# Loads moved and spread at two places of a hybrid mLSTM and attention decode step: gate columns, constants and sinks at the start, the samples' attention in the middle

## The chip, the cores and the metric

The kernel runs on one core of a Trainium2 chip. The metric is device time in microseconds (us), the median over runs. The engines named below are TensorE (PE for its products, PEld for its weight loads), VectorE (DVE), ScalarE (ACT), GpSimd (POOL) and SyncE (SP, which here issues most DMAs). Each engine runs its own instructions in a fixed order.

## The reference

One layer of a decoder works on 512 prompt tokens and on 8 sampled sequences of 4 tokens: 544 columns of x, each of width 2048. It projects x with one large matrix, runs two branches (an mLSTM with 4 heads of 512, and sliding-window attention with 32 query heads and 4 key heads of 64), gates and merges them and ends in a layer norm:

```
u = einsum('btd,dc->btc', x, w_in)         # q_m k_m v_m o_m z_m q_a k_a v_a z_a g_m g_a i_pre f_pre
ig = i_pre + b_igate ; lf = log_sigmoid(f_pre + b_fgate)
h_m, C, n, m = mlstm(q_m, k_m, v_m, ig, lf, C0, n0, m0)
h_a = softmax([q_a k_a - slope*dist, sink]) v_a      # window of 128; samples read the stored K and V too
br_m = norm(h_m) * sigmoid(o_m) * silu(z_m) ; br_a = h_a * silu(z_a)
y = sigmoid(g_m) * (br_m @ w_proj_m) + sigmoid(g_a) * (br_a @ w_proj_a)
out = layernorm(ALPHA * x + y @ w_out)
```

It also returns the mLSTM states and the new K and V rows, for the prompt and for the samples. i_pre and f_pre, the gate columns, are the last 8 columns of w_in.

## The kernel before

All values are float32. Each operand of a product is split into a high part, a cast to the format that TensorE takes, and a low part, the rest (`split` for weights, lines 193 to 203: the cast on ScalarE at line 200, the subtraction on VectorE at line 201; `hilo` for x and other data, lines 243 to 245). Three products (high by high, high by low, low by high) make one.

**The start.** x comes in five column blocks on SP (line 306), with two halves of the first weights between them (`load_half`, line 187); a third half follows. The 16 slices of x are called pieces here, k = 0 to 15. Each piece is turned by four transposes on TensorE (line 324) and split by `hilo`; for k below 8 a copy (line 331) goes with it. The samples' x lies in the tile `xs`, of which half is used. Then SP issues seven small loads (lines 360 to 366): the rest of the constants `cc`, the two biases, the state m0, the norm's weights, and the attention sinks in two layouts. ScalarE casts parts of the constants into `sel` and `m8r` (lines 369 and 376). Two plain products follow (`gemm`, the attention's values, columns VA_ and VA_ + 128); between the halves of the second, `gates_half` loads 8 gate columns into a tile of the three-buffer weight pool (line 381), casts them twice on ScalarE (lines 386, 387), subtracts on VectorE (line 388) and multiplies (line 393).

**The pairs.** Most of the time goes to `paired`. A pair is two column blocks of weights, worked out together by a scheme with seven half products instead of eight (lines 668 and 670, `half_product`: 16 and 8 products of 272 columns). The seven operands of x are called a11, s1, n2, xk, n3, s4, xk. The weights of a step are prepared three steps ahead.

**Ticks.** Everything beside the pairs is written as generators, held in a list. After each half product `tick()` lets every generator run to its next `yield`; a `yield` thus means "go on one step later". Instructions that a tick issues on TensorE are placed behind the half product just issued. `tc.issue_after(ins)` asks for such a place: what is issued in its block on the engine of `ins` stands behind `ins` there. `state["load"]`, `state["cast"]` and `state["split"]` hold the latest weight load (SP), weight cast (ScalarE) and weight subtraction (VectorE). `tc.high_priority` lets a block be placed ahead of what was written before it. For the rest a planner orders each engine's instructions by what is ready in its own estimate of time.

**From the samples' attention to the attention branch.** `attentions` runs the 16 prompt attentions, then `sample_attention`. It issues 13 loads in a row: z (gas), new keys (kas), values (vas), eight pieces of q (qraw, lines 912 to 918), and the stored K and V (kb and vb, 1 MB each, lines 922 and 923). It yields five times, scales q (line 932), transposes the keys (line 939) and goes on. When it is done, `samples` works through four mLSTM heads of the samples, each a fixed number of yields: eight rounds (line 1226 reads the state, line 1231 updates it) and a tail, `sample_finish`: a product (line 1177), a norm, transposes (line 1184) and a store (line 1186). Right behind the last tail `samples` gives its memory free and loads the 16 blocks of the attention branch into the tiles `pf` (line 1261). When the pairs are done, `branch` splits these blocks (bh and bl, by `hilo`), and the products with w_proj_a begin (line 210).

Of the kernel before, what the change touches and what calls it, by code (L numbers as in the profile page):

```python
# [15 lines left out]
F32 = mybir.dt.float32  # L16
# [58 lines left out]
def _build(tc, nc, i, o, es):  # L75
# [25 lines left out]
    def nm(s):  # L101
        count[0] += 1
        return f"{s}_{count[0]}"
# [120 lines left out]
    def gemm(wv, c0, xh, xl, cols=EVEN, raws=(None, None), every=8, prio=0, before=None, parts=(1, 1),  # L224
             ps=None):
        ps = ps or mm()
        for half in range(2):
            if before:
                before(half)
            raw = raws[half] or load_half(wv, c0, half)  # L230
            if prio:
                with tc.high_priority(offset=prio):
                    wh, wl = split(raw, parts=parts[half])
            else:
                wh, wl = split(raw, parts=parts[half])
            products(ps, half, wh, wl, xh, xl, cols, every)
        return ps
# [5 lines left out]
    def hilo(src, hi, lo, eng=None):  # L243
        A.copy(hi, src)
        (eng or V).tensor_tensor(out=lo, in0=src, in1=r32(hi), op=ALU.subtract)
# [66 lines left out]
    state["load"] = xdma  # L312
    with tc.issue_after(xdma.ins):
        raw0.append(load_half(win, VA_ + 128, 0))
# [4 lines left out]
    for g in range(8):  # L319
        for q in range(2):  # L320
            k = g * 2 + q
            pt = sm()
            for t in range(4):
                PE.transpose(pt[:, t * 128:t * 128 + 128], xt[k][:, t], ident)
# [34 lines left out]
    with tc.issue_after(state["load"].ins):  # L359
        nc.sync.dma_start(cc[:, 128:C_DIST], i["consts"][:, 128:C_DIST])  # L360
        nc.sync.dma_start(bi[:, 0:1], i["b_igate"].unsqueeze(1))
        nc.sync.dma_start(bi[:, 1:2], i["b_fgate"].unsqueeze(1))
        nc.sync.dma_start(m0, i["state_mlstm_m"].rearrange("b h -> h b"))
        nc.sync.dma_start(wn[:], i["mlstm_norm_w"].rearrange("(a p) -> p a", p=128))
        nc.sync.dma_start(sinkb[:], i["attn_sinks"].partition_broadcast(128))
# [3 lines left out]
    A.copy(sel[:], cc[:, C_SEL:C_SEL + 32])  # L369
# [5 lines left out]
    for q in (0, 2):  # L375
        A.copy(m8r[q * 32:q * 32 + 32], cc[q * 32:q * 32 + 32, C_M8:C_M8 + 8])


    def gates_half(ps, half):
        raw = wr.tile([128, 8, 128], F32, tag="raw", name=nm("graw"))  # L380
        nc.sync.dma_start(raw[:, :, 0:8], win[:, half * 8:half * 8 + 8, GI:GI + 8])
        wa, wb = gate_w
        for g in range(2):
            src = raw[:, :, g * 4:g * 4 + 4]
            hi = wa[:, :, g * 32:g * 32 + 4]
            A.copy(hi, src)
            A.copy(wb[:, :, g * 32:g * 32 + 4], src)
            V.tensor_tensor(out=wa[:, :, 64 + g * 32:68 + g * 32], in0=src, in1=r32(hi), op=ALU.subtract)
# [516 lines left out]
    def sample_attention():  # L905
# [9 lines left out]
        for kvh in range(KVH):  # L915
            half = slice((kvh % 2) * 64, (kvh % 2) * 64 + 64)
            for a in range(2):
                nc.sync.dma_start(qraw[half, kvh // 2, a::2],
                                  d_qa[kvh * 4:kvh * 4 + 4, a * 64:a * 64 + 64].rearrange("k p t -> p k t"))
        kb = t1.tile([128, NB, 256], F32, name="kb")  # L920
        vb = t1.tile([128, NB, 256], F32, name="vb")
        nc.sync.dma_start(kb[:], i["state_attn_k"].rearrange("b t k d -> t b (k d)"))
        nc.sync.dma_start(vb[:], i["state_attn_v"].rearrange("b t k d -> t b (k d)"))
# [986 lines left out]
```

## Time and profile before

| | |
|---|---|
| Time, median of 3 runs | 2465.89 us (2465.31 to 2469.09) |
| Profiled execution, own time | 2469.53 us |
| Its span | 2467.7 us |
| Granted TensorE clock, mean | 0.997 |
| PE busy | 2436.4 us (99%) |
| PEld busy | 2379.8 us (96%) |
| DVE busy | 1876.5 us (76%) |
| ACT busy | 1216.6 us (49%) |
| POOL busy | 509.8 us (21%) |
| Data moved | 464.72 MB, mean 188 GB/s |

A row of the order of time gives the start in us, the duration, the engine, the line in the kernel, the operation, the tile written and the tiles read, the shape, and the count of merged instructions; in brackets stands how long the engine had been idle and what it waited for. SPq marks DMA issues on SP, whose duration is that of the issue, not of the transfer. A row of waits gives who waited for whom, the total in us, the number of times and the longest. A row of stretches gives start and end, the length, the busy time and number of instructions of each engine, the granted clock (1.00 is full), the DMA engines' busy share and GB/s. Durations of products overlap, since the engine is pipelined: two products of 272 columns start 0.125 us apart though each shows 0.29 us.

### The profile page before, as it was taken

How to read it: one execution, taken by the hardware profiler on the slowest of the kernel's cores; microseconds unless marked ns; L12 is line 12 of the kernel's file. 1: busy time of each engine (PE TensorE's matmuls, PEld its weight loads, DVE VectorE, ACT ScalarE, POOL GpSimd, SP SyncE). 2: the span in 40 equal slices, each digit the busy share in tenths (PEclk: the TensorE clock that was granted, in tenths of full speed). 3: DMA queues.
4: the chain of work that ended last, by engine and by line, in shares of the span. 5: the costliest groups of instructions: out<-in, count | busy, mean ns of one | idle time of the engine just before them, and what ended most of it. 6: DMA issues, size and time to landing. Idle time of an engine off the chain costs nothing.

```text
span 2467.7 us, 48808 instructions
## 1 busy us (share of the span) xinstructions
PE 2436.4 (99%) x19446; PEld 2379.8 (96%) x19446; DVE 1876.5 (76%) x2813; ACT 1216.6 (49%) x1994; POOL 509.8 (21%) x478
## 2 busy tenths in 40 slices
PE   8999999999999999999999999999999999999997
PEld 8999999999999999999999999999999999999996
DVE  7868888888888887787877878877866654777657
ACT  5456676676576664443433544544633333334431
POOL 3114333333333330121012122111000000110111
PEclk9999999999999999999999999999999999999998
DMA  6776666666666645477678577677755546888875
GB/s 170 192 180 158 164 157 152 158 154 162 154 151 169 151 121 144 122 214 237 192 240 243 177 230 227 180 237 229 243 196 171 178 153 204 227 224 253 222 217 179
DMA packets 557435, 464.72 MB, mean 188 GB/s; under 512 B 45592, under 2 KB 454344, under 8 KB 556952
## 3 DMA queue, kind: packets, MB, share of 16 engines
q1 hardware_dynamic: 540312, 402.09, 54.8%
q0 software_dynamic: 15696, 57.15, 12.1%
q8 instruction: 153, 2.51, 0.4%
q10 hardware_dynamic: 1200, 2.36, 0.3%
q14 instruction: 74, 0.61, 0.1%
HBM read 319.06 MB, written 96.31 MB: 168 GB/s over the span
## 4 chain that ended last, share of the span: by engine, by line
PE 92%; DMA 3%; DVE 2%; SPq 1%; issue 1%; ACT 0%; DVEq 0%; POOL 0%; POOLq 0%
PE bank L668 45%; PE bank L670 22%; PE bank L210 10%; PE sm L1414 2%; PE bank L1226 1%; PE sm L1446 1%; PE sm L778 1%; PE sm L1459 1%; PE sm L824 1%; PE sm L210 1%; DMA tx<-d_y 1%; DMA ty<-d_y 1%; PE sm L1776 1%; DMA raw<-in_w_in 1%; PE sm L804 1%
## 5 line engine op out<-in xcount | busy, mean ns | idle before, releaser
L200 ACT CAST wh<-raw 128x1024 fp32r<-128x1024 f32 x632 | 662.5, 1048 | 843.7 <-PE bank L668 690.1
L201 DVE TENSOR_TENSOR wl<-raw,wh 128x1024 fp32r<-128x1024 f32 x632 | 788.6, 1249 | 203.4 <-ACT wh L200 177.4
L668 PE MATMUL bank<-xk,wh 128*128 128x272 f32 x2336 | 322.7, 289 | 0.0
L648 DVE TENSOR_TENSOR raw<-raw,raw 128x1024 f32<-128x1024 f32 x238 | 302.4, 1271 | 8.3 <-DMA raw<-in_w_in 4.3
L668 PEld LDWEIGHTS bank<-xk,wh 128*128 128x128 f32 x2336 | 302.8, 188 | 3.5 <-issue 2.6
L687 POOL TENSOR_TENSOR ev<-p,ev 128x272 f32<-128x272 f32 x82 | 119.2, 1454 | 435.2 <-ACT ev L686 412.5
L668 PE MATMUL bank<-n3h,wh 128*128 128x272 f32 x656 | 169.5, 291 | 1.6 <-DVE ev L689 1.6
L670 PE MATMUL bank<-xk,wl 128*128 128x272 f32 x1168 | 169.6, 287 | 0.0
L668 PE MATMUL bank<-n2h,wh 128*128 128x272 f32 x656 | 169.5, 291 | 0.0
L668 PE MATMUL bank<-s1h,wh 128*128 128x272 f32 x656 | 169.2, 291 | 0.0
L668 PE MATMUL bank<-n2l,wh 128*128 128x272 f32 x656 | 167.8, 287 | 0.0
L668 PE MATMUL bank<-n3l,wh 128*128 128x272 f32 x656 | 167.7, 288 | 0.0
L668 PE MATMUL bank<-s1l,wh 128*128 128x272 f32 x656 | 167.2, 287 | 0.0
L668 PE MATMUL bank<-s4h,wh 128*128 128x272 f32 x656 | 167.1, 288 | 0.0
L668 PE MATMUL bank<-s4l,wh 128*128 128x272 f32 x656 | 166.8, 287 | 0.0
L670 PEld LDWEIGHTS bank<-xk,wl 128*128 128x128 f32 x1168 | 155.5, 188 | 0.0
L668 PE MATMUL bank<-a11h,wh 128*128 128x272 f32 x584 | 150.3, 289 | 0.0
L668 PE MATMUL bank<-a11l,wh 128*128 128x272 f32 x584 | 149.6, 288 | 0.0
L210 PE MATMUL bank<-bh,wl 128*128 128x272 f32 x704 | 148.5, 289 | 0.0
L210 PE MATMUL bank<-bh,wh 128*128 128x272 f32 x704 | 148.0, 289 | 0.0
L210 PE MATMUL bank<-bl,wh 128*128 128x272 f32 x704 | 146.0, 288 | 0.1
L646 POOL DMA_DIRECT2D raw<-raw x90 | 78.5, 873 | 287.0 <-DVE ev L695 209.8
(492 smaller groups left out, 5668.5 us busy)
## 6 DMA issues: line engine op xcount, KB each, us to landing
raw<-in_w_in SPq DMA_DIRECT2D x296, 512.0 KB
raw<-raw POOLq DMA_DIRECT2D x90, 512.0 KB, 5.0
C<-in_state_mlstm_C SPq DMA_DIRECT2D x32, 1024.0 KB
out<-C SPq DMA_DIRECT2D x64, 512.0 KB
raw<-in_w_proj_a SPq DMA_DIRECT2D x32, 512.0 KB
raw<-in_w_proj_m SPq DMA_DIRECT2D x32, 512.0 KB
raw<-in_w_out SPq DMA_DIRECT2D x32, 512.0 KB
d_v<-ev SPq DMA_DIRECT2D x16, 272.0 KB
```

The lines of the kernel that those rows point to most:

```text
L200: state["cast"] = A.copy(wh[:, k:k + n], raw[:, k:k + n])
L201: state["split"] = V.tensor_tensor(out=wl[:, k:k + n], in0=raw[:, k:k + n], in1=r32(wh[:, k:k + n]), op=ALU.subtract)
L210: PE.matmul(ps[f][:, :w], a[:, kk], b(k, c, w), start=(k == 0 and n == 0), stop=(k == 15 and n == 2))
L646: G.dma_start(out=w[out][:], in_=w[b][:], accum_op=ALU.add)
L648: V.tensor_tensor(out=w[out][:], in0=w[a][:], in1=w[b][:], op=ALU.add)
L668: PE.matmul(ps, wh[:, k], x(p, k), start=(first and k == 0 and p == 0), stop=False, skip_group_check=True)
L670: state["end"] = PE.matmul(ps, wl[:, k], x(0, k), start=False, stop=(k == 7), skip_group_check=True)
L687: G.tensor_tensor(out=c22, in0=p1, in1=c11, op=ALU.subtract)
L778: PE.matmul(pp[:, c0 + w0:c0 + 256], qs[a][:, j * 128:j * 128 + 128], kx[:, k0:k0 + 256 - w0], start=(n == 0), stop=(n == 1))
L804: PE.transpose(pt[:, b * 128:b * 128 + 128], s_[:, b, 128:256], ident)
L824: PE.matmul(po[:, b * 128:b * 128 + n], VA[:, b], p_[:, 2 * b:2 * b + n // 128], start=(b == 0 and m == 0), stop=(b == 3 and m == 1), skip ...
L1414: PE.matmul(pp[:, 0:258], a[:, b * 128:b * 128 + 128], b_[:, b, f], start=(b == 0 and n == 0), stop=(b == 3 and n == 2))
```

## The change

1. The gate columns get a place in the unused half of `xs`. Both loads are issued behind the last block of x and ahead of the third weight half. The gate casts on ScalarE are placed behind the last cast of x.
2. The seven small loads and the casts into `sel` and `m8r` move into a generator, `small_loads`, started after the first plain product: biases, m0 and constants in its first tick, the norm's weights and the sinks three ticks later, the casts three ticks after that. Each is placed behind the latest weight load or weight cast.
3. The first weight cast on ScalarE is placed behind the cast of the piece k = 3.
4. The 13 loads of the samples' attention are spread: kas, vas and gas at once; one pair of q loads in each of the next four ticks; kb and vb in later ticks; then q is scaled, and the key transposes follow two ticks after that. Every load is placed behind the latest weight load, the scaling behind the latest weight subtraction. From the first load to the key transposes there are ten yields, where there were five.

```diff
@@ gemm
-                wh, wl = split(raw, parts=parts[half])
+                with tc.issue_after(behind.ins) if behind and half == 0 else ExitStack():
+                    wh, wl = split(raw, parts=parts[half])
@@ hilo
-        A.copy(hi, src)
+        state["x_cast"] = A.copy(hi, src)
@@ loads of x
+    graw = blk(xs[:, 4], 2)
     with tc.issue_after(xdma.ins):
+        for half in range(2):
+            nc.sync.dma_start(graw[:, half].rearrange("p (k c) -> p k c", c=8), win[:, half * 8:half * 8 + 8, GI:GI + 8])
         raw0.append(load_half(win, VA_ + 128, 0))
@@ pieces of x
+                if k == 3:
+                    state["k3"] = state["x_cast"]
...
+                x_cast = state["x_cast"]
@@ small loads
-    with tc.issue_after(state["load"].ins):
-        nc.sync.dma_start(cc[:, 128:C_DIST], i["consts"][:, 128:C_DIST])
...
-        nc.sync.dma_start(sinkc[:], i["attn_sinks"].unsqueeze(1).to_broadcast([AH, NTS]))
-    A.copy(sel[:], cc[:, C_SEL:C_SEL + 32])
+    def small_loads():
+        with tc.issue_after(state["load"].ins):
+            nc.sync.dma_start(bi[:, 0:1], i["b_igate"].unsqueeze(1))
+            nc.sync.dma_start(bi[:, 1:2], i["b_fgate"].unsqueeze(1))
+            nc.sync.dma_start(m0, i["state_mlstm_m"].rearrange("b h -> h b"))
+            nc.sync.dma_start(cc[:, 128:C_DIST], i["consts"][:, 128:C_DIST])
+        for _ in range(3):
+            yield
+        with tc.issue_after(state["load"].ins):
+            nc.sync.dma_start(wn[:], i["mlstm_norm_w"].rearrange("(a p) -> p a", p=128))
+            nc.sync.dma_start(sinkb[:], i["attn_sinks"].partition_broadcast(128))
+            nc.sync.dma_start(sinkc[:], i["attn_sinks"].unsqueeze(1).to_broadcast([AH, NTS]))
+        for _ in range(3):
+            yield
+        with tc.issue_after(state["cast"].ins):
+            A.copy(sel[:], cc[:, C_SEL:C_SEL + 32])
...
@@ gates_half
-        raw = wr.tile([128, 8, 128], F32, tag="raw", name=nm("graw"))
-        nc.sync.dma_start(raw[:, :, 0:8], win[:, half * 8:half * 8 + 8, GI:GI + 8])
+        raw = graw[:, half].rearrange("p (k c) -> p k c", c=8)
...
-            A.copy(hi, src)
-            A.copy(wb[:, :, g * 32:g * 32 + 4], src)
+            with tc.issue_after(x_cast.ins):
+                A.copy(hi, src)
+                A.copy(wb[:, :, g * 32:g * 32 + 4], src)
@@ plain products
-                  before=gates_between if kk else None, ps=[sm(), sm()] if kk else None)
+                  before=gates_between if kk else None, ps=[sm(), sm()] if kk else None, behind=state["k3"])
...
+            spawn(small_loads())
@@ sample_attention
-        nc.sync.dma_start(gas[:], d_bra[:, :, SEQ:T].rearrange("k p t -> p k t"))
-        nc.sync.dma_start(kas[:], d_ka[:, :, SEQ:T].rearrange("k p t -> p k t"))
-        nc.sync.dma_start(vas[:], d_vr[SEQ:T])
...
+        with tc.issue_after(state["load"].ins):
+            nc.sync.dma_start(kas[:], d_ka[:, :, SEQ:T].rearrange("k p t -> p k t"))
+            nc.sync.dma_start(vas[:], d_vr[SEQ:T])
+            nc.sync.dma_start(gas[:], d_bra[:, :, SEQ:T].rearrange("k p t -> p k t"))
...
-        for _ in range(5):
-            yield
-        for j in range(2):
-            V.tensor_scalar(qas[:, j], qraw[:, j].rearrange("p g (b t) -> p b g t", t=NTS), 0.125, None, op0=ALU.mult)
+        for kvh in range(KVH):
+            half = slice((kvh % 2) * 64, (kvh % 2) * 64 + 64)
+            yield
+            with tc.issue_after(state["load"].ins):
+                for a in range(2):
+                    nc.sync.dma_start(qraw[half, kvh // 2, a::2],
+                                      d_qa[kvh * 4:kvh * 4 + 4, a * 64:a * 64 + 64].rearrange("k p t -> p k t"))
+        for t_, src in ((kb, i["state_attn_k"]), (vb, i["state_attn_v"])):
+            yield
+            with tc.issue_after(state["load"].ins):
+                nc.sync.dma_start(t_[:], src.rearrange("b t k d -> t b (k d)"))
+            yield
+        with tc.issue_after(state["split"].ins):
+            for j in range(2):
+                V.tensor_scalar(qas[:, j], qraw[:, j].rearrange("p g (b t) -> p b g t", t=NTS), 0.125, None, op0=ALU.mult)
+        for _ in range(2):
+            yield
```

More of the change, by code (lines that the diff above doesn't have):

```diff
@@ L224, in gemm @@
     def gemm(wv, c0, xh, xl, cols=EVEN, raws=(None, None), every=8, prio=0, before=None, parts=(1, 1),
-             ps=None):
+             ps=None, behind=None):
         ps = ps or mm()
@@ L357, in t5 @@
         return t544.tile([128, n], dt, tag="t544", name=nm("t"))
-    with tc.issue_after(state["load"].ins):
-        nc.sync.dma_start(cc[:, 128:C_DIST], i["consts"][:, 128:C_DIST])
[L361 to L365, printed above, removed]
-        nc.sync.dma_start(sinkc[:], i["attn_sinks"].unsqueeze(1).to_broadcast([AH, NTS]))
     G.memset(mh[:], -0.5)
     V.tensor_scalar(ones_r[:], cc[:, 0:2], 0.0, 0.5, op0=ALU.mult, op1=ALU.add)
-    A.copy(sel[:], cc[:, C_SEL:C_SEL + 32])
     for t_ in (row_h, nM):
@@ L374, in _build @@
     V.memset(r32(m8r[:]), 0.0)
-    for q in (0, 2):
-        A.copy(m8r[q * 32:q * 32 + 32], cc[q * 32:q * 32 + 32, C_M8:C_M8 + 8])
+    def small_loads():
[14 more added lines that the diff above has]
+            A.copy(sel[:], cc[:, C_SEL:C_SEL + 32])
+            for q in (0, 2):
+                A.copy(m8r[q * 32:q * 32 + 32], cc[q * 32:q * 32 + 32, C_M8:C_M8 + 8])
     def gates_half(ps, half):
-        raw = wr.tile([128, 8, 128], F32, tag="raw", name=nm("graw"))
-        nc.sync.dma_start(raw[:, :, 0:8], win[:, half * 8:half * 8 + 8, GI:GI + 8])
+        raw = graw[:, half].rearrange("p (k c) -> p k c", c=8)
         wa, wb = gate_w
@@ L911, in sample_attention @@
         vas = t1.tile([32, 256], F32, name="vas")
-        nc.sync.dma_start(gas[:], d_bra[:, :, SEQ:T].rearrange("k p t -> p k t"))
-        nc.sync.dma_start(kas[:], d_ka[:, :, SEQ:T].rearrange("k p t -> p k t"))
-        nc.sync.dma_start(vas[:], d_vr[SEQ:T])
[L915 to L919, printed above, removed]
+        with tc.issue_after(state["load"].ins):
+            nc.sync.dma_start(kas[:], d_ka[:, :, SEQ:T].rearrange("k p t -> p k t"))
+            nc.sync.dma_start(vas[:], d_vr[SEQ:T])
+            nc.sync.dma_start(gas[:], d_bra[:, :, SEQ:T].rearrange("k p t -> p k t"))
         kb = t1.tile([128, NB, 256], F32, name="kb")
         vb = t1.tile([128, NB, 256], F32, name="vb")
-        nc.sync.dma_start(kb[:], i["state_attn_k"].rearrange("b t k d -> t b (k d)"))
-        nc.sync.dma_start(vb[:], i["state_attn_v"].rearrange("b t k d -> t b (k d)"))
         E = t1.tile([128, NB, 132], F32, name="E")
```

## The prediction

> **What bounds the kernel now.** I read the page's totals first, then a table of stretches, then the waits of TensorE, then the order of time on single engines around each place the diff touches.
>
> ```profile
> span 2467.7 us, 48808 instructions
> PE 2436.4 (99%) x19446; PEld 2379.8 (96%) x19446; DVE 1876.5 (76%) x2813; ACT 1216.6 (49%) x1994; POOL 509.8 (21%) x478
> ```
>
> TensorE is busy in all but 31.3 us of the span, so a change that keeps its products can win only where TensorE stands idle, and loses wherever a new idle stretch opens. The stretches (columns: length, busy time of PE, PEld, DVE, ACT, POOL, granted clock, DMA share, GB/s) say where the idle time lies:
>
> ```profile
> 8.00:12.20 4.20, 2.74 (x21) 2.27 (x19) 0.49 (x2) 1.51 (x3) 0.00 (x0) 1.00 1.08 366
> 12.20:20.00 7.80, 7.02 (x54) 6.62 (x55) 6.47 (x18) 7.05 (x25) 6.19 (x5) 1.00 1.10 350
> 20.00:30.00 10.00, 6.59 (x51) 5.90 (x50) 6.04 (x14) 4.58 (x18) 5.06 (x4) 1.00 0.36 35
> 40.00:50.00 10.00, 10.00 (x82) 10.00 (x82) 10.00 (x18) 4.11 (x8) 0.00 (x0) 1.00 0.54 144
> ...
> 920.00:930.00 10.00, 9.69 (x78) 9.51 (x77) 5.11 (x7) 3.55 (x4) 1.41 (x1) 1.00 0.53 123
> 930.00:940.00 10.00, 9.05 (x99) 8.70 (x98) 5.25 (x7) 2.03 (x4) 0.00 (x0) 1.00 1.11 317
> 940.00:950.00 10.00, 9.15 (x132) 8.39 (x134) 8.87 (x14) 6.56 (x14) 2.97 (x2) 1.00 0.30 90
> ...
> 1760.00:1765.00 5.00, 4.94 (x39) 4.67 (x38) 4.59 (x8) 4.97 (x9) 0.00 (x0) 1.00 1.02 378
> ```
>
> In reach of the change are 1.46 + 0.78 + 3.41 = 5.65 us at the start and 0.31 + 0.95 + 0.85 = 2.11 us at the attention of the samples, 7.8 us together. That is the ceiling of the gain. The last row is a place where nothing is idle yet; it will matter.
>
> **The start: ScalarE without foreign waits.** The order of time on ScalarE and on SP:
>
> ```profile
> 8.78 0.39 ACT L244 CAST a11h<-sm 128x272 fp32r<-128x272 f32 x1 [3.43 <-PE sm L324]
> 11.07 1.04 ACT L200 CAST wh<-raw 128x1024 fp32r<-128x1024 f32 x1 [1.91 <-DMA raw<-in_w_in]
> 12.55 0.69 ACT L244 CAST a11h<-sm 128x272 fp32r<-128x272 f32 x2
> 24.64 0.22 ACT L369 CAST sel<-cc 128x32 fp32r<-128x32 f32 x1 [2.00 <-DMA cc<-in_consts]
> 28.78 0.22 ACT L386 CAST wg<-graw 128x32 fp32r<-128x32 f32 x1 [3.12 <-DMA graw<-in_w_in]
> ...
> 25.20 1.13 SPq L381 DMA_DIRECT2D graw<-in_w_in  x2
> ```
>
> Casts of x queue on ScalarE behind the cast of sel (2.00 us for the constants) and the gate casts (3.12 us for the gate columns, which SP issues behind the constants and the sinks, at 25.20). TensorE pays:
>
> ```profile
> PE bank L210 <- ACT xk L244: 3.0, 2, 2.4
> PE bank L210 <- ACT wh L200: 1.4, 1, 1.4
> PE bank L210 <- ACT a21h L244: 0.8, 1, 0.8
> ```
>
> After the change the gate loads leave SP ahead of the third weight half, and the sel, m8r and gate casts stand behind the last cast of x. The 3.0 us go; I take 3.2 of the 3.41 in the stretch from 20 to 30.
>
> The first cast of weights moves behind the fourth piece of x. Today it holds ScalarE from 9.17 to 12.1 while casts of x are ready. Ahead of it then come eight casts and three copies, at 0.33 us each (two take 0.69 in the row at 12.55): from 8.78 to 12.4, then 1.04 for the weights, so the first product starts near 13.4 instead of 12.1. That costs 1.3; the 0.8 us wait for a21h then goes, since those casts are done. I take +0.2, since transposes of the next pieces can fill part of the wait; ends -1.5 (all of it filled) and +1.3. Start in all: -3.0, between -4.9 and -1.7 (then 3.0 gained at the late end).
>
> Other loads. The rows for what hides them:
>
> ```profile
> 59.72 0.48 DVE L412 SCALAR_TENSOR_TENSOR t<-bank,bi,t 4x272 f32<-4x272 f32 x1
> 61.62 0.29 PE L668 MATMUL bank<-n2h,wh 128*128 128x272 f32 x1
> L388 DVE TENSOR_TENSOR wg<-graw,wg x4: 174/184/193, 29.0 to 42.9; 128x32 fp32r<-128x32 f32 x4
> ```
>
> The seven small DMAs are issued later, the two gate loads some 13 us earlier: the same count on SP. The first three are issued in the first tick of the second value product, and the bias is first read at 59.72: hidden. If it came late, VectorE's weight subtractions would queue behind that add and TensorE would wait for as long. The third weight half stands behind 1.13 us of gate issue and is cast only after x: nothing. The gate tile leaves the three-buffer pool, so the next weights load earlier; TensorE is full there (10.00 of 10.00), so nothing is gained. In exchange the tile of x_sample stays taken until the last gate subtraction (42.9), and the first b22 can be loaded only then. It is used first in the third step of the first pair, at 61.62, and prepared some 4 us ahead: 14 us for a load, hidden. If that cover went, the pair would stall by the excess.
>
> **The samples' attention.** TensorE's longest wait there:
>
> ```profile
> PE sm L939 <- DMA kb<-in_state_attn_k: 0.9, 1, 0.9
> ```
>
> The thirteen loads stand in a block on SP today, with the next weights behind them. Spread, with kb issued several ticks before its first transpose, the 0.9 and the weights' lateness go. I take -1.5 of the 2.11, between -2.1 and 0.
>
> **The price: five more ticks.** Before, five yields separate the loads from the first scaling of q; after, four (q) + four (kb, vb) + two = ten. One tick follows each seventh of a pair, and everything behind (the four sample heads, then the 16 loads of the attention branch, line 1261) is counted in ticks with no wait between that could swallow five: the heads' operands are done pairs ahead. So the end of the samples moves five steps against the pairs, which do not move. On TensorE:
>
> ```profile
> 1708.41 1.06 PE L1226 MATMUL bank<-C,qz 128*32 128x512 f32 x8
> 1728.03 1.06 PE L1226 MATMUL bank<-C,qz 128*32 128x512 f32 x8
> 1738.59 0.39 PE L1177 MATMUL sm<-rep,sel 128*32 128x512 f32 x1
> 1751.67 0.43 PE L1184 MATMUL sm<-cc,w 32*128 32x32 f32 x4
> 1753.63 1.17 PE L670 MATMUL bank<-n3h,wl 128*128 128x272 f32 x8
> 1756.63 1.16 PE L670 MATMUL bank<-s4h,wl 128*128 128x272 f32 x8
> 1759.63 1.15 PE L670 MATMUL bank<-xk,wl 128*128 128x272 f32 x8
> 1760.76 0.50 PE L210 MATMUL bank<-bh,wh 128*128 128x272 f32 x2
> ```
>
> A step is 3.0 us (1753.63 to 1756.63). The last two rounds of the samples lie six steps apart (19.6 = 6 x 3.0 + 1.5), just as the loop's yields say. L1177 stands behind the last step of the last pair but one. Five steps on, it stands behind n3 of the last pair: 1738.59 + 15.0 = 1753.6. Then comes the tail of the last head:
>
> ```profile
> 1752.85 0.37 SPq L1186 DMA_DIRECT2D d_brm<-gs  x1
> 1753.82 10.45 SPq L1261 DMA_DIRECT2D pf<-d_bra  x16
> ...
> 1757.78 0.64 ACT L244 CAST bh<-pf 128x544 fp32r<-128x544 f32 x1
> 1759.32 0.72 DVE L245 TENSOR_TENSOR bl<-pf,bh 128x544 fp32r<-128x544 f32 x1
> ...
> 1753.00:1758.00 5.00, 1.74 (x3) 1.00 0.91 262
> 1738.00:1750.00 12.00, 10.59 (x16) 1.00 0.13 45
> ```
>
> The branch tiles reuse the samples' memory, so their loads start 2.15 us after L1184, and the next product (1760.76) needs the first of them, 6.2 us after the issue (bl ends at 1760.04). Today this ends as the pairs end: no slack is left. From L1177 to L1184 it is 13.1 us now, with VectorE 10.59 of 12.00 us busy (last two rows, VectorE alone); at its new place VectorE is 1.74 of 5.00 us busy, and L1184 must follow s4 of the last pair (1757.6). I estimate 6 us for the chain, nearer the idle row: L1184 at 1759.8, loads at 1762.0, first product some 5 us later (no weight cast ahead of the branch cast) at 1767, against 1760.76: 6.2 us of idle TensorE. Ends: 1757.8 + 2.15 + 4.6 gives 3.8; the old 13.1 with 2.15 and 6.2 gives 14.2.
>
> An idle stretch has a second price. In the kernel's tail, after some microseconds with few products:
>
> ```profile
> 2425.00:2430.00 5.00, 4.73 (x26) 4.40 (x25) 4.81 (x10) 0.00 (x0) 0.00 (x0) 0.66 0.96 365
> 2427.09 0.68 PE L210 MATMUL sm<-yh,w 128*128 128x288 f32 x2
> 2428.97 0.43 PE L210 MATMUL sm<-yh,w 128*128 128x288 f32 x2
> ```
>
> The granted clock falls to 0.66 in that stretch, and two products take 0.68 instead of 0.43 us for about 2 us: some 1.0 us lost. I add 1.0, between 0 and 2; less 0.2 for quicker loads. The lost stretch is +7.0, between 3.6 and 16.
>
> [...]
>
> **Sum.** -3.0 (start) - 1.5 (attention) + 7.0 (branch loads) = +2.5 us. The profiled execution took 2469.53 us, 3.6 above the median of 2465.89 and past the slowest of the three; the sum would put it at 2472.0. Runs are compared by medians, so I forecast 2465.89 + 2.5 = 2468.4. 0.2% is 4.9 us, about what a measurement of this kernel can tell from no change; the forecast is within it.
>
> **Rivals.**
>
> Hidden branch loads (faster side). If the loads at 1261 wait for nothing of the samples' tail, or the five ticks are swallowed, only the gains stay: 2465.89 - 4.5 = 2461.4. For it: 13 us pass from L1177 to L1184 with little work of its own. Against it: the loads start 0.97 us after the head's store, all 16 in a row. It decides once the price is under 2 us. On the edge of 0.2%, so half of it counts as faster. Chance 0.17.
>
> The old tail. If the chain takes its 13.1 us again, L1184 comes at 1766.7 and the loss is 14 + 1 us: 2465.89 - 4.5 + 15 = 2476.4. It makes the kernel slower by over 0.2% from a price of 9.4 us up. For it: the same instructions on in-order engines; against it, the emptier VectorE. Chance 0.21.
>
> No gain at the start. If the later weight cast leaves TensorE without products and x is late for other reasons, the start gives 0: 2465.89 - 1.5 + 7.0 = 2471.4, just slower. For it: DMA is full (350 GB/s) until 20 us. Against it: DMA moves 35 GB/s from 20 to 30, while TensorE waits. Chance 0.10.
>
> **How the numbers follow.** The forecast has 0.52, the rivals 0.17, 0.21 and 0.10. The likeliest case's own range is 2464.5 to 2472. To reach 8 in 10 the range goes to both outer cases: 2461.0 to 2476.5. Faster: half of the first rival and a little of the forecast's lower end, 0.12. Slower: the second, most of the third and the forecast's upper end, 0.36. Same: 0.52.
>
> **What would show it.** Right: no wait of ScalarE for constants or gate columns; TensorE idle below 0.5 us from 20 to 30; no wait for kb; L1177 behind n3 of the last pair; branch loads after the pairs' last product; an idle stretch of 4 to 8 us, with a clock below 1.00, near 1755 to 1765. Wrong: branch loads ahead of the last pair's end; a first product later than 14 us; a pair waiting for b22; or new idle time in the pairs.

## The result and the profile after

The changed kernel takes 2480.28 us, the median of six runs (2478.05 to 2481.90), beside 2466.06 us for the kernel before in six runs of the same session (2465.31 to 2469.09). The ratio is 1.0055, with a 95% interval from 1.0042 to 1.0068: slower by 14 us, well over the 0.2% that can be told from no change. The forecast was 2468.4 us in a range up to 2476.5, so the result lies past even the rival of the old tail.

The profiled execution of the changed kernel took 2479.81 us, close to its median, where that of the kernel before lay 3.5 us above its own. The spans therefore differ by 10.2 us and the medians by 14.2. The first lines of the page after:

```profile
span 2477.9 us, 48814 instructions
PE 2439.2 (98%) x19446; PEld 2383.8 (96%) x19446; DVE 1880.0 (76%) x2813; ACT 1219.8 (49%) x1996; POOL 504.6 (20%) x478
```

TensorE is idle for 38.7 us (2477.9 - 2439.2) in place of 31.3, and it is busy for 2.8 us longer with the same 19446 products: some of them ran slower. The table of stretches says where both come from (columns as in the prediction: length, busy time of PE, PEld, DVE, ACT, POOL, granted clock, DMA share, GB/s):

```profile
20.00:30.00 10.00, 9.50 (x80) 9.28 (x79) 9.35 (x20) 8.26 (x20) 5.87 (x5) 1.00 0.65 136
940.00:950.00 10.00, 10.00 (x134) 9.67 (x133) 5.00 (x11) 3.79 (x7) 0.00 (x0) 1.00 0.46 132
960.00:970.00 10.00, 6.57 (x43) 6.35 (x42) 3.15 (x6) 8.46 (x22) 2.78 (x2) 0.83 0.07 28
1760.00:1765.00 5.00, 1.19 (x10) 0.88 (x8) 3.98 (x9) 0.62 (x1) 0.00 (x0) 1.00 1.07 375
1765.00:1770.00 5.00, 0.00 (x0) 0.00 (x0) 0.00 (x0) 0.27 (x1) 0.00 (x0) 0.53 0.80 235
1770.00:1775.00 5.00, 4.39 (x15) 3.55 (x16) 2.45 (x4) 2.36 (x5) 0.00 (x0) 0.50 0.95 308
```

The two gains are there: 20 to 30 went from 6.59 to 9.50 us of busy TensorE, and 940 to 950 is full. Two idle stretches are new, one near 965 that nobody expected, and the one after the pairs, which is twice as long as forecast. The order of time on TensorE around the second:

```profile
1751.53 0.40 PE L1201 MATMUL sm<-rep,sel 128*32 128x512 f32 x1
1756.99 1.15 PE L687 MATMUL bank<-xk,wl 128*128 128x272 f32 x8
1759.05 0.44 PE L1208 MATMUL sm<-cc,w 32*128 32x32 f32 x4 [0.91 <-ACT w L1076]
1770.43 0.82 PE L210 MATMUL bank<-bh,wh 128*128 128x272 f32 x2 [9.24 <-ACT bh L245]
1774.48 0.65 PE L210 MATMUL bank<-bh,wh 128*128 128x272 f32 x2
1779.22 0.41 PE L210 MATMUL bank<-bh,wl 128*128 128x272 f32 x2
```

(L1201 and L1208 are the lines 1177 and 1184 of before, L1210 and L1285 the lines 1186 and 1261, L687 the line 670.) Between the pairs' last step and the first branch product there are 13.44 us, where there were 1.13 (1760.76 - 1759.63). The last two rows show the clock: two products take 0.65 in place of 0.41. And SP in the same time:

```profile
1748.99 2.27 SPq L1502 DMA_DIRECT2D t<-d_v  x4
1753.78 1.85 SPq L1502 DMA_DIRECT2D t<-d_k  x4
1756.72 2.30 SPq L1502 DMA_DIRECT2D t<-d_q  x3
1760.74 0.91 SPq L1311 DMA_DIRECT2D d_sga<-ev  x1
1761.74 0.39 SPq L187 DMA_DIRECT2D raw<-in_w_proj_a  x1
1762.22 2.68 SPq L1210 DMA_DIRECT2D d_brm<-gs  x1
1764.95 10.32 SPq L1285 DMA_DIRECT2D pf<-d_bra  x13
```

The twelve loads t of the mLSTM, 3 MB in all, now stand ahead of the head's store and of the branch loads. Before, the branch loads came first (1753.82) and nearly all of t from 1766.8 on. The issues of t are themselves over at 1759.02, just ahead of the head's transposes at 1759.05. Most of what lies between the transposes and the branch loads is the slow issue of the two stores behind t: d_sga takes 0.91 us and gs 2.68 us, where the kernel before has 0.32 and 0.37.

A ledger, which divides each profiled span into four parts, makes all the kernels here comparable. The marks are the third pair's first block of low weights (a11h,wl, 102.25 before and 96.50 after), the pairs' last xk,wl, the first branch product and the end of the span. Before to after: start -5.75, pairs with the samples' attention +3.11, wait for the branch +12.31, the rest +0.5; sum +10.2. That is 4.0 us less than the medians differ by, because the profile of the kernel before is a long one: by the ledger of all kernels below, its start is 1.2 us later than the mean of the five kernels with that start, and its last part is 2.1 us longer than the mean of the six kernels with early branch loads. One wait of TensorE belongs to the old start: the row below has its like (1.3 to 1.6 us) in four of the five profiles with that start, and in none of the nine with the new start is such a wait longer than 0.43 us at that place.

```profile
91.14 0.37 PE L668 MATMUL bank<-n3h,wh 128*128 128x272 f32 x1 [1.32 <-DVE ev L689]
```

### The profile page after: what moved, and what is told of

Its sections match the earlier page's. It is cut to its first block, busy times and chain, and to the rows that moved or that the text cites. A ratio compares the mean times of both kernels' runs of the same rounds, so it can differ in the third digit from the quotient of the medians.

```text
span 2477.9 us, 48814 instructions
## 1 busy us (share of the span) xinstructions
PE 2439.2 (98%) x19446; PEld 2383.8 (96%) x19446; DVE 1880.0 (76%) x2813; ACT 1219.8 (49%) x1996; POOL 504.6 (20%) x478
## 5 line engine op out<-in xcount | busy, mean ns | idle before, releaser
L687 PE MATMUL bank<-xk,wl 128*128 128x272 f32 x1168 | 170.3, 288 | 0.0
L687 PEld LDWEIGHTS bank<-xk,wl 128*128 128x128 f32 x1168 | 156.4, 189 | 0.1
```

The costliest lines, as they stand in the source:

```text
L687: state["end"] = PE.matmul(ps, wl[:, k], x(0, k), start=False, stop=(k == 7), skip_group_check=True)
```

## The experiments

The theory after the result, T: the five extra ticks alone make the loss. Rivals: the late start of the casts pushes something on (R1), or the spread loads themselves collide (R2). Two kernels do one half of the change each, one does the whole change in the old number of ticks, one does the ticks alone.

**Start only.** Parts 1 to 3 of the change, with the samples' loads in their old block (the edit is against the changed kernel, and shortened):

```diff
-        with tc.issue_after(state["load"].ins):          # kas, vas, gas; then q, kb, vb over ten ticks
+        nc.sync.dma_start(gas[:], ...)                   # the 13 loads in a row, as before
+        for _ in range(5):
+            yield
```

> Parts 1 to 3 of the change without the spread loads of the attention. Theory T (the five extra ticks push the branch loads behind the pairs): these parts only gain, 4 to 6 us, about 2460 to 2462 us, and the branch loads start about 8 us ahead of the pairs' end as before. Rival R1 (the moved small loads and the earlier weight loads upset something later): no gain or a loss, 2466 us or more.

Measured: 2463.34 us, ratio 0.9985 (0.9976 to 0.9995). R1 falls: the start gains, by a little less than the 4 to 6 us forecast.

**Attention only.** Part 4 on the kernel before (shortened):

```diff
-        nc.sync.dma_start(gas[:], ...)                   # the 13 loads in a row, five yields
+        with tc.issue_after(state["load"].ins):          # spread over ten ticks, as in the change
```

> Part 4 of the change alone on the kernel before. Theory T: the whole loss and more is here, 2480 to 2486 us, with an idle stretch of about 10 us at the first product of the branch. Rival R1: about 2464 to 2466 us, the loads' spread being a small gain.

Measured: 2484.24 us, 1.0075 (1.0060 to 1.0090), as theory T forecast. TensorE is idle for 9.25 us ahead of the first branch product.

**The whole change in five ticks.**

```diff
         for kvh in range(KVH):
-            yield
+            if kvh % 2 == 0:
+                yield
...
                 nc.sync.dma_start(t_[:], src.rearrange("b t k d -> t b (k d)"))
-            yield
...
-        for _ in range(2):
-            yield
+        yield
```

> The whole change, but the spread loads take five ticks as the block did (two key heads of q in each of two ticks, then K, V and the scaling). Theory T: the idle stretch behind the pairs goes and only the gains stay, 2458 to 2462 us. Rival R2 (the spread itself and the places behind weight loads cost, whatever the number of ticks): 2476 us or more.

Measured: 2463.04 us, 0.9985 (0.9976 to 0.9995). The idle stretch behind the pairs is gone. A wait of 1.4 us for kb is left.

**The kernel before with ten yields.**

```diff
-        for _ in range(5):
+        for _ in range(10):
             yield
```

> The kernel before with ten yields in place of five behind the block of loads, nothing else. Theory T: the same loss as with the change, without its gains: 2478 to 2486 us. Rival R2: 2464 to 2468 us, as before, since neither loads nor casts have moved.

Measured: 2487.56 us, 1.0088 (1.0073 to 1.0103). Theory T holds: one number, with no load moved, makes the kernel 21 us slower, and the same loads spread over five ticks cost nothing. R2 falls too. The next kernels take the loss apart.

**The branch loads ahead of t.** The changed kernel, where the twelve first loads of t wait for the last branch load to be issued:

```diff
-            nc.sync.dma_start(st[:], d_bra[k])
+            state["pf"] = nc.sync.dma_start(st[:], d_bra[k])
...
-            nc.sync.dma_start(t_[:], d_[h * 4 + c][:, 0:SEQ])
+            with tc.issue_after(state["pf"].ins):
+                nc.sync.dma_start(t_[:], d_[h * 4 + c][:, 0:SEQ])
```

> The changed kernel, with the mLSTM's twelve first loads of t placed behind the last of the sixteen branch loads on SP; nothing else differs. Theory Q (the queue): the 3 MB of t ahead of the store of gs and the branch loads cost the branch about 5 us (5.9 us from the head's last transposes to the first branch load, against 2.15 before). Then the branch loads start near 1761.5, the first branch product comes 4 us earlier than in the changed kernel, and the time is 2475 us, between 2473 and 2477, against 2480.3. Rival L (only the tail's lateness): the gs store waits for its product and the loads of t cost nothing, so the time stays within 1 us of 2480.

Measured: 2476.02 us, 1.0036 (1.0022 to 1.0050), 4.7 us under the changed kernel by the ratios, though the two intervals overlap at their ends (1.0042 to 1.0068 there). Its order of time on SP, and then on TensorE:

```profile
1760.44 0.39 SPq L1210 DMA_DIRECT2D d_brm<-gs  x1
1761.54 10.97 SPq L1285 DMA_DIRECT2D pf<-d_bra  x16
```

```profile
1759.51 0.43 PE L1208 MATMUL sm<-cc,w 32*128 32x32 f32 x4 [0.91 <-ACT w L1076]
1766.90 0.82 PE L210 MATMUL bank<-bh,wh 128*128 128x272 f32 x2 [6.96 <-ACT bh L245]
1770.09 0.57 PE L210 MATMUL bank<-bh,wh 128*128 128x272 f32 x2
1770.50 0.41 PE L210 MATMUL bank<-bl,wh 128*128 128x272 f32 x2
```

Theory Q holds, and the trace shows it better than the time: with t behind, the store issues in 0.39 us again, and the branch loads stand 2.03 us behind the head's transposes, where the changed kernel had 5.9.

**Forty transposes in the idle stretch.** They fill the wait, and shorten nothing:

```diff
+        warm = sm()
+        with tc.issue_after(state["tail"].ins):          # the last head's transposes
+            for _ in range(40):
+                PE.transpose(warm[:, 0:128], ident, ident)
         esS.close()
```

> The changed kernel, with forty transposes of the identity (0.22 us each in the start's row, 8.8 us together) on TensorE behind the last head's transposes; their result is used by nothing. They fill the idle stretch before the first branch product without making it shorter. Theory C (the clock): the half-rate products from 1770.4 to 1778.6 cost about 4 us, so the granted clock stays at 1.00 there and the time is 2476.5 us, between 2475 and 2478. Rival F (fed by the loads): the products of those microseconds wait for branch tiles at any clock, since sixteen tiles take some 11 us to come; then the clock is 1.00, TensorE idles instead, and the time stays within 1 us of 2480.

Measured: 2481.49 us, 1.0058 (1.0043 to 1.0073). This was no test: the forty took 4.59 us, 0.11 each, not 0.22, left an idle stretch of 5.3 us and a clock of 0.50 behind it.

**Seventy-six transposes.** The same with `range(76)`.

> As the run with forty transposes, which took 4.59 us in place of 8.8 and left 5.3 us of idle TensorE ahead of the first branch product, with 76 of them: 8.7 us, from the head's last transposes to about 1769.5, with the mLSTM's transposes behind. Theory C: the clock stays at 1.00 from 1770 on and the time is 3 to 4 us under the changed kernel's ratio of 1.0055, 1.004. Rival F: the products then wait for branch tiles at full clock, and the ratio stays within 0.0005 of 1.0055.

Measured: 2482.68 us, 1.0060 (1.0046 to 1.0074), no gain. Its order of time on TensorE:

```profile
1761.14 8.52 PE L1284 MATMUL sm<-cc 128*128 128x128 f32 x76
1770.18 1.04 PE L1421 MATMUL sm<-cc,t 128*128 128x128 f32 x8
1773.62 0.52 PE L210 MATMUL bank<-bh,wh 128*128 128x272 f32 x2 [2.40 <-ACT bh L245]
1774.38 0.52 PE L210 MATMUL bank<-bl,wh 128*128 128x272 f32 x2 [0.24 <-DVE bl L246]
1775.92 0.82 PE L210 MATMUL bank<-bh,wh 128*128 128x272 f32 x2 [0.68 <-ACT bh L245]
1781.80 0.41 PE L210 MATMUL bank<-bh,wh 128*128 128x272 f32 x2
```

The first branch products do run at full clock (0.52, as the 0.50 of before), then wait for the next branch tile, as rival F says, and then the granted clock falls to 0.50 all the same, from about 1775 to about 1781.7. So the two causes were not separated. What the ledger gives is their sum: from the first branch product to the end of the span it is 707.0 us on average in the eight kernels whose branch loads are late (705.7 to 707.7) and 704.8 in the six where they are not (703.5 to 706.9). The two groups overlap. By their means half clock and late tiles together cost some 2.2 us; how much of it is clock stays open.

**Seven yields.** The kernel before with `range(7)`.

> The kernel before with seven yields instead of five ahead of the samples' attention, nothing else. Ten yields gave 2487.6, 21 us above the kernel before. If every tick costs alike once the slack is zero (theory T, linear), two cost 8.4 us: 2475 us, between 2472 and 2477. Rival S (the tail shortens first): the last head's chain takes less time at a place where VectorE is less busy, and the store and the loads stay ahead of the mLSTM's loads, so two ticks cost 3 us or less: 2467 to 2470.

Measured: 2483.26 us, 1.0066 (1.0051 to 1.0081). Both forecasts fell: two ticks cost 16 us, where five cost 21. By the ledger below, 11.5 us of the 16 and 12.7 of the 21 are the wait for the branch: that part of the price is a step. Its order of time on SP:

```profile
1754.48 1.86 SPq L1478 DMA_DIRECT2D t<-d_v  x3
1762.15 0.39 SPq L1186 DMA_DIRECT2D d_brm<-gs  x1
1767.88 11.85 SPq L1261 DMA_DIRECT2D pf<-d_bra  x16
```

The last head's store goes out 9.3 us later than before (1752.85), and by then other issues stand ahead of the branch loads: five more of t, a store of the pairs (d_sga) and two other loads lie between the two last rows.

The other 4.2 of the 16 us lie in the pairs, and most of them in one stall that the kernel before does not have:

```profile
1607.85 0.71 PE L1231 MATMUL sm<-VB,Ab 32*128 32x512 f32 x4 [2.56 <-DMA VB<-d_kv]
```

TensorE waits for a load of the last head, VB, whose issue on SP comes at 1601.05, 10.6 us later than before (1590.48). From 1600 to 1620 the granted clock is 0.91.

**Seven yields, branch loads ahead of t.** The kernel of seven yields with the edit of the branch loads from above.

> The kernel before with seven yields in place of five, and the mLSTM's twelve loads of t behind the branch loads on SP. Seven yields alone gave 2483.3, 16 us over the kernel before, with the head's last transposes at 1760.0, the first branch load at 1767.9 and the first branch product at 1775.1. Theory Q: nearly all of that is the order on SP. The branch loads start 2.1 us behind the head's last transposes, at 1762.1, the first product comes 4.7 us later at 1766.8, against 1763.5 where the pairs end: 3.3 us of idle time and up to 1.6 us of clock, 2470 to 2473. Rival: the late tail itself costs it, and the time stays above 2478.

Measured: 2481.58 us, 1.0056 (1.0041 to 1.0071). Theory Q as I had put it falls: by the ratios some 2 us come back of 16, not 11, and the intervals of the two kernels overlap so far that even these are not certain. TensorE and then SP:

```profile
1759.90 0.43 PE L1184 MATMUL sm<-cc,w 32*128 32x32 f32 x4
1762.37 1.18 PE L670 MATMUL bank<-xk,wl 128*128 128x272 f32 x8
1772.64 0.82 PE L210 MATMUL bank<-bh,wh 128*128 128x272 f32 x2 [9.09 <-ACT bh L244]
```

```profile
1762.09 0.66 SPq L1186 DMA_DIRECT2D d_brm<-gs  x1
1764.74 0.33 SPq L1287 DMA_DIRECT2D d_sga<-ev  x1
1765.65 11.63 SPq L1261 DMA_DIRECT2D pf<-d_bra  x16
```

With t out of the way the store of the pairs' last result (d_sga) stands ahead of the branch loads. It can leave only when ScalarE has finished that result (1764.06 plus 0.66), and the branch loads wait behind it. Their memory should have been free by then, since before and with the branch loads ahead of t they went out 1.0 to 1.1 us behind the store of gs, and here 3.6 us. The first tile then takes 6.3 us from its issue to its cast (1765.65 to 1771.94), against 4.7 with the branch loads ahead of t; and the stall for VB is here, too (3.18 us). In every kernel with a late tail the branch loads start behind the pairs' end, with two more ticks as with five. I take this for the reason of the step; no run moves the store of d_sga by itself.

**Ten ticks, five taken out behind.** The changed kernel, with five yields removed after the exps of the samples' attention, so that the heads are back at their old ticks:

```diff
-        for _ in range(3):
-            yield
...
         for b2_ in range(4):
             yield
-            yield
+            if b2_ > 1:
+                yield
             for _ in before:
```

> The changed kernel, with five yields taken out behind the exps of the samples' attention (three ahead of the first transposed weights, one in each of two rounds), so that the samples' heads stand at their old ticks while the loads stay spread over ten. Theory T+E (two separate losses): the branch loads are back ahead of the pairs' end and the late start goes, while the exps still stand ahead of a weight cast near 960 us and cost 3 us: 2465 us, between 2464 and 2467. Rival T alone (the stall near 960 costs nothing at the end): 2462 us, between 2460.5 and 2463.5. If the ticks at the heads are not what counts, it stays near 2480.

Measured: 2465.35 us, 0.9989 (0.9979 to 0.9998). The late branch loads are gone with the five yields (16.3 us by the two ratios). The time lies in the range of theory T+E, and a stall near 965 us is left. In the changed kernel it looks like this on ScalarE:

```profile
958.07 1.28 ACT L992 ACT_TABLE_LOAD   x1
959.37 0.41 ACT L992 ACTIVATE E<-E,sast 128x132 f32<-128x132 f32 x1
962.11 1.28 ACT L1302 ACT_TABLE_LOAD   x1
963.40 0.66 ACT L1302 ACTIVATE ev<-ev 128x544 f32<-128x544 f32 x1
964.08 1.28 ACT L992 ACT_TABLE_LOAD   x1
966.26 1.03 ACT L200 CAST wh<-raw 128x1024 fp32r<-128x1024 f32 x1
```

and on TensorE:

```profile
967.34 4.00 PE L685 MATMUL bank<-xk,wh 128*128 128x272 f32 x16 [3.43 <-ACT wh L200]
971.13 2.02 PE L687 MATMUL bank<-xk,wl 128*128 128x272 f32 x8
```

The eight exps of the softmax stand in one row on ScalarE with a sigmoid of the pairs among them. Three loads of activation tables, 1.28 us each, stand in that row, and the next weight cast waits until 966.26. TensorE is idle for 3.43 us and then starts at half clock (0.50 from 967 to 973): sixteen products take 4.00 in place of 2.16 us.

In the kernel with five ticks taken out the exps again stand with a sigmoid among them and three table loads, and the next weight cast waits until 968.55. But what ends TensorE's wait there is the sums of the softmax on VectorE, since three of the yields taken out stood between the exps and the products that read them:

```profile
968.90 0.49 PE L1007 MATMUL sm<-cc,En 128*32 128x128 f32 x2 [2.49 <-DVE sast L997]
```

So theory T+E holds as to a second, smaller loss, and only in part as to its cause.

**Twelve ticks, seven taken out.** The same with two more yields ahead and two more out behind. The exps then come one whole pair of seven steps later than before, at their old place within the pair:

```diff
-        for _ in range(2):
+        for _ in range(4):
             yield
...
         for b2_ in range(4):
             yield
-            if b2_ > 1:
-                yield
             for _ in before:
```

> The whole change with twelve yields ahead of the attention (seven more than before, which is one whole pair) and seven taken out behind the exps, so the heads stand at their old ticks and the exps at the old place within a pair, one pair later. Theory A (alignment): the exps again follow a weight cast as in the kernel before, the stall of 3.4 us near 960 goes, no wait for kb is left, and the ratio is 0.998, 1 to 2 us under the kernel with ten ticks and five out (0.9989). Rival: the stall belongs to the exps at any later place (a sigmoid and its table loads fall among them), and the ratio stays at 0.9989.

Measured: 2458.88 us, 0.9969 (0.9958 to 0.9980), 8 us under the kernel before. It is the lowest ratio of all, though its interval overlaps those of the four other kernels below 1. Its ScalarE has one table load ahead of the exps, and the next weight casts follow at 966.03:

```profile
961.24 1.28 ACT L992 ACT_TABLE_LOAD   x1
962.53 0.41 ACT L992 ACTIVATE E<-E,sast 128x132 f32<-128x132 f32 x1
966.03 1.98 ACT L200 CAST wh<-raw 128x1024 fp32r<-128x1024 f32 x2
```

and its stretch of the samples' attention is full:

```profile
900.00:1000.00 100.00, 99.98 (x869) 95.24 (x868) 74.60 (x105) 50.99 (x84) 14.08 (x10) 1.00 0.48 131
```

In the kernel before TensorE is busy for 97.90 us of that stretch, in the changed one for 96.57 at a clock of 0.97. Theory A holds: what costs is where the exps meet the pair's own work on ScalarE. All fourteen profiles agree with this. In seven, those with ten yields ahead of the exps (changed, attention only, ten yields, branch loads ahead of t, both runs with transposes, and ten ticks with five out), TensorE loses some 3 us near 965: it is busy for 6.57 to 7.28 us of the ten from 960 to 970, and in attention only and ten yields for 36.6 of the forty from 960 to 1000. In the ledger below their pairs take 1659.6 us or more. In the other seven it is busy there for 9.98 us of the ten or more, or for 40.00 of the forty, and the pairs take 1658.2 us or less, but for the two kernels with seven yields and their stall for VB. On ScalarE the changed kernel and ten ticks with five out have a sigmoid among the exps and three table loads; before and twelve ticks with seven out have one table load ahead of them. That the sigmoid among the exps is the cause was not tried by itself.

**Keys first.** The whole change in five ticks, with kb ahead of q:

```diff
+            nc.sync.dma_start(kb[:], i["state_attn_k"].rearrange("b t k d -> t b (k d)"))
         for kvh in range(KVH):
...
+            nc.sync.dma_start(gas[:], d_bra[:, :, SEQ:T].rearrange("k p t -> p k t"))
+            nc.sync.dma_start(vb[:], i["state_attn_v"].rearrange("b t k d -> t b (k d)"))
```

> The whole change with the spread loads in five ticks and kb's load ahead of those of q, gas and vb. The same spread with kb behind q gave 0.9985 of the kernel before and kept 1.4 us of waiting for kb on TensorE. Theory T: the ticks are as before, so nothing is late, and the wait for kb goes: 1.4 us less than that, 0.9979, some 5 us under the kernel before. Rival: another load takes its place (q behind 1 MB of kb, or the weights behind both) and the ratio stays at 0.9985.

Measured: 2462.56 us, 0.9984 (0.9975 to 0.9993). The ratio stays where the rival had it, though the two forecasts lie only 0.0005 apart, less than the interval can tell. The trace has the reason: no wait for kb is left, but one of 1.3 us for VectorE's work on the scores takes its place. It is not a load, as the rival had thought.

The ledger of all kernels, from one profile each (us):

| kernel | third pair's first step | from there to the pairs' last step | to the first branch product | from there to the end | ratio |
|---|---|---|---|---|---|
| before | 102.25 | 1657.4 | 1.1 | 706.9 | 1 |
| changed | 96.50 | 1660.5 | 13.4 | 707.5 | 1.0055 |
| start only | 96.90 | 1658.2 | 1.1 | 704.5 | 0.9985 |
| attention only | 101.03 | 1661.6 | 13.4 | 705.7 | 1.0075 |
| five ticks | 96.84 | 1657.7 | 1.1 | 706.0 | 0.9985 |
| before, ten yields | 100.67 | 1665.6 | 13.9 | 707.7 | 1.0088 |
| branch loads ahead of t | 96.91 | 1660.5 | 9.5 | 707.0 | 1.0036 |
| forty transposes | 97.48 | 1660.9 | 13.9 | 707.6 | 1.0058 |
| before, seven yields | 100.92 | 1661.5 | 12.6 | 706.9 | 1.0066 |
| ten ticks, five out | 98.79 | 1659.6 | 1.1 | 703.5 | 0.9989 |
| keys first | 96.61 | 1657.1 | 1.1 | 703.7 | 0.9984 |
| seventy-six transposes | 98.40 | 1660.3 | 14.9 | 707.5 | 1.0060 |
| twelve ticks, seven out | 96.65 | 1655.0 | 1.1 | 704.4 | 0.9969 |
| seven yields, branch ahead | 100.36 | 1662.0 | 10.3 | 706.3 | 1.0056 |

## Why the prediction was wrong

Two steps of the prediction failed. The price of the branch loads took the 2.15 us from the head's transposes to their first issue over from their old place, and it was 5.9; and the attention's term of -1.5 left out that the five ticks move the softmax, which turned it into +3.1. The changed kernel's trace shows the first, and the run with twelve ticks and seven out the second.

**The start, -3.0: right, and a little small.** Start only is 0.15% faster, 3.7 us, though its interval reaches from 1.2 to 5.9. In the ledger the third pair's first step comes at 101.0 on average in the five kernels with the old start and at 97.2 in the nine with the new one, 3.8 us earlier. The first product came at 13.01 where I had put 13.4. One term was off without harm: the two gate loads took SP 4.77 us to issue, not 1.13, in a stretch where DMA was full (share 1.10 from 11.2 to 16 us), and the third weight half was late by a wait of 1.00 us on ScalarE. No wait for the small loads or for the first b22 appeared, and from 20 to 30 us TensorE was idle for 0.50 us.

**The samples' attention, -1.5: wrong as it stood, +3.1.** The 2.11 us of idle time went, as forecast. What I did not cost is that the five ticks move the attention's own work, too, against the pairs' work on ScalarE. I followed the moved heads and left out the moved softmax, which lies nearer. "New idle time in the pairs" was one of the signs of being wrong, and it came. The moved softmax cost 3.43 us of idle TensorE and, from the two rows above, 4.00 + 2.02 us for products that take 2.16 + 1.16 elsewhere, some 2.7 us more. Those two and the 2.1 gained make +4.0 where the ledger shows +3.1; the remaining 0.9 I have not followed. With the exps at a better place in the pair (twelve ticks, seven out) the term is 1655.04 - 1657.38 = -2.3.

**The branch loads, +7.0: right in mechanism, mis-sized.** The runs put it, with the clock behind it, at 16.3 us (changed against ten ticks, five out), the ledger at 12.3 of waiting and some 2.2 behind it. The prediction's own ladder shows the step that failed. It was made on the clock of before, so the changed kernel's rows are moved by 2.64 us, by which its pairs end earlier (1759.63 - 1756.99):

| mark | predicted | measured, moved | error so far |
|---|---|---|---|
| the head's product (L1177, now L1201) | 1753.6 | 1754.2 | 0.6 |
| the head's transposes (L1184, now L1208) | 1759.8 | 1761.7 | 1.9 |
| first branch load issued | 1762.0 | 1767.6 | 5.6 |
| first branch product | 1767 | 1773.1 | 6.1 |

The place behind n3 of the last pair was right, the tail's chain took 7.5 us against 6, and from the issue to the product it was 5.5 against 5. The term that failed is the 2.15 us from L1184 to the branch loads, taken over from the old place: it was 5.9, and makes 3.7 of the error of 6.1. The queue of SP was read at the place the loads left, not at the place they came to. There the mLSTM's loads and the pairs' end stores are ready first, and a late load stands behind them and behind their slow issue (0.91 and 2.68 us for the two stores). With t put behind, the same steps took 2.03 us and then 5.36 to the first product, as forecast.

**The clock, +1.0: too small by about one.** The half clock lasts much longer than I took from the kernel's tail (1770.4 to 1778.9, 8.5 us), but the products of that time would partly wait for branch tiles anyway (0.68 us ahead of the second tile with seventy-six transposes), and the whole stretch costs some 2.2 us by the means of the ledger. Its length was not the same everywhere. With the branch loads ahead of t it lasted from 1766.90 to about 1770.4, 3.5 us of unbroken products, and in the changed kernel 8.5 us there and 6.0 us of unbroken products after the stall near 965. With seventy-six transposes the longest idle stretch ahead was 2.40 us, and the clock fell to 0.50 all the same.

**The rivals.** The chain did not take its old 13.1 us (7.5), so that rival fell; its time was reached and passed by another way, the queue. The rival of no gain at the start fell with the first run, and that of hidden branch loads with the result. The upper bound of 16 us for the branch loads was nearly right by itself (16.3 by the runs); the range failed because the attention came out on the other side of nothing, 4.6 us off, on top of the 6.1. That with no slack even two ticks would cost most of the price, I had not seen.

**The baseline.** I worked with differences against the profiled execution, whose start was 1.2 us later than the mean of the five with that start. The start's gain in the traces is so made to look larger (5.75) than the runs say (3.7), and its last part was long as well, so that the +0.5 of the rest hides most of the 2.2 us behind the branch loads.

## What to carry to other kernels

A yield added to one generator moves everything behind it in that generator against everything else: list each moved piece, the nearest first, and for each ask what it meets on its engine at the new place. For a load that comes late, read the queue at its new place: what is ready earlier there goes ahead, and the price can be a step, as here, and not a slope. Where a delay is wanted for its own sake, take as many ticks out behind it, and choose their number so that bursts of ScalarE work keep their place within the period.

## What the runs showed of the hardware

The clock fell to half (0.50 from 1775 to 1780) after a stretch that was only thin, not empty: with seventy-six transposes there were six products between 1771.2 and 1775.9, and no gap over 2.40 us. The clock at the start differs from profile to profile: in three of the fourteen it was 0.79 from 12 to 20 us rather than 1.00, with either start. Two of them have the new start, and their third pair begins at 98.4 and 98.8, where the other seven lie between 96.5 and 97.5. The third has the old start, and there the lower clock cost nothing that the ledger shows: its 100.36 is the earliest of the five. The stretch with seventy-six transposes, and then with keys first:

```profile
12.00:20.00 8.00, 7.31 (x48) 7.34 (x49) 5.64 (x11) 6.01 (x20) 6.62 (x5) 0.79 1.08 317
```

```profile
12.00:20.00 8.00, 7.37 (x61) 7.40 (x62) 6.18 (x13) 6.48 (x22) 7.32 (x6) 1.00 1.08 319
```

TensorE is busy as long in both, with 48 and 61 products. A DMA's issue on SP is not of fixed cost in these traces either: the store of gs took 0.37 us before and 2.68 us behind all twelve loads of t. What makes it slow is open. Behind seven of the twelve (seven yields) it took 0.39 us, and a store of d_sga took 0.32 us at 1765.42 in the kernel before, in a stretch where DMA was full (share 1.05, 1765 to 1770).
